# The folded pairs of a ConvFFN, written out by hand for four engines, with weight buffers in separate pools

## The chip, the core and the metric

The kernel runs on one core of a Trainium2 chip. The metric is the time of one execution on the device, in microseconds; several executions are timed and their median is taken. TensorE is called PE below (PEld is its weight load), VectorE DVE, ScalarE ACT, GpSimd POOL and SyncE SP. SP does nothing but issue loads and stores here; POOL does some arithmetic and issues the accumulating transfers named below.

## The reference

It is a trunk of two layers with width 1024 on one sequence of 512 positions. Each layer has a token mixer (retention in layer 0, mLSTM in layer 1) and a channel mixer, the ConvFFN, both behind an RMSNorm whose shift, scale and gate come from a vector `c`. The change is in the ConvFFN of layer 1, the last mixer before the final norm.

```python
D_MODEL, SEQ, DEPTH, D_FF, FFN_CONV = 1024, 512, 2, 2816, 3

def conv_ffn(h, w_up, conv_w, conv_b, w_down):
    u = causal_dwconv(h @ w_up, conv_w, conv_b)        # 5632 columns, three taps in time
    a, b = jnp.split(u, 2, axis=-1)
    return (jax.nn.silu(a) * b) @ w_down

for i in range(DEPTH):
    ...
    x = x + gt_t * mixer(h)
    h = rmsnorm(x, norm_ffn_g[i]) * (1.0 + sc_f) + sh_f
    x = x + gt_f * conv_ffn(h, ffn_w_up[i], ffn_conv_w[i], ffn_conv_b[i], ffn_w_down[i])
return rmsnorm(x, final_g)
```

## The kernel before

**Arithmetic.** Every large product is taken in three parts. A float32 matrix is split into a rounded high part and a remainder, its low part, and PE multiplies high by high, high by low and low by high (`mm3`, L231 to L233). A weight arrives as a tile of 128x1024 floats, `raw`, 512 KB, loaded on SP's queue. ACT casts it into `whi` (L155) and DVE subtracts that from `raw` into `wlo` (L160). There is a second way to a low part, `low_part_added`: ACT writes minus `whi` into `wlo` (L166), and a DMA on POOL's queue adds the weight to it (L167).

**Straight pairs and folded pairs.** The up-projection has 44 tiles of 128 columns; tile f and tile f + 22 make a pair, since the Silu of the one gates the other. A straight pair is two chains of 24 matmuls over 512 positions. A folded pair is worked out as a matrix of 2x2 blocks with seven block products in place of eight: a product is 12 matmuls over 256 positions, so a pair has 84 of them. The seven need sums of the two weight tiles (`wa`, `wb` give `ws` and `wt`, L205 to L208 on DVE), the same kind of sums of `h` (made once, in `turn`), and additions afterwards. `c1` and `c2` are two PSUM banks of 128x512. Three times ACT copies half of `c2` out: `s[HA]` after product 1 (L348), `s[HB]` after product 6 (L339), `q` after product 7 (L343), and DVE adds a copy into a bank (L340, L344, and the one behind product 3). Product 6 accumulates onto what product 1 left in `c2`, so it can't start ahead of the copy of `s[HA]`; product 7 stands so to the copy of `s[HB]`, and product 4 to the addition of `q` (L344). Products 1 and 2 take the parts of `wa`, 5 and 7 those of `ws`, 6 and 3 those of `wt`; product 4 takes `bp`, a tile that holds the high and the low part of half of `wb` side by side.

**What follows a pair.** For each of its two tiles ACT starts the convolution out of the bank (L748) and DVE adds two taps (L750). Then ACT takes the Silu (L760), DVE multiplies the halves (L761), ACT casts the result into `ggh` (L227) and DVE subtracts for `ggl` (L228). This is called the gate of a pair here. The down-projection runs in pieces over groups of 4, 4, 4, 4 and 6 pairs; a piece is one tile of `w_dn` with 24 matmuls over 512 positions in two halves of 12, each followed by the addition to the residual x (L419).

**Order.** The program is a list of items, each with the weights that it uses. Weights go out up to four items ahead, as long as a budget of tiles allows. All tiles of weights, whatever they hold, come from one pool, `wts`, of 22 buffers that go round in turn: a buffer is given out again once its last reader is done. Pairs 0 to 3 are straight and 4 to 21 folded (`FOLD_FROM`). A folded pair is an item of its own, `fold_item`, called a unit here; in 16 of the 18 units a piece of `w_dn` is run between the products (`down`, from the second unit on). Inside a unit PE's order is that of the code. The order on ACT, DVE and POOL is set by the scheduler, which ranks ready instructions by their place in the program. The unit's parameter `prepare` holds the steps for the next fold: `step_a` (parts of `wa`, all sums), `step_b` (parts of `ws`), `step_c` (parts of `wt`, with the accumulating DMA in every second fold), `step_d` (`bp`), and last the load of the fold after next. The last group of six is run behind all units by `boundary`, in two halves of the positions, with the final norm beside it.

Of the kernel before, what the change touches and what calls it, by code (L numbers as in the profile page):

```python
# [9 lines left out]
F32 = mybir.dt.float32  # L10
# [17 lines left out]
NWT = 22  # L28
BUDGET = 16
BUDGET_FOLD = 20  # L30
FOLD_FROM = 4
# [8 lines left out]
NSLOTS = 58  # L40
# [30 lines left out]
def trunk(ctx: ExitStack, tc: tile.TileContext, xT, cb, pos, vec, decay, zmask, ada, w_s0, w_in0, w_v0,  # L71
# [4 lines left out]
    wts = ctx.enter_context(tc.tile_pool(name="wts", bufs=NWT))  # L76
# [13 lines left out]
    def wide(s, dt=F32):  # L90
        return wts.tile([P, WCOLS + WPAD], dt, tag="w", name=s)
# [21 lines left out]
    c_ext = const.tile([P, D + 1], F32, tag="c", name="c_ext")  # L113
# [8 lines left out]
    V.memset(const.tile([P, 32], F32, tag="pad2", name="pad2")[:], 0.0)  # L122
# [47 lines left out]
    class Chunk:  # L170
        tiles = 2

        def __init__(self, src, n, off):
            raw, r = wide(uid("raw")), slice(0, n)
            nc.sync.dma_start(raw[:, r], src)
            self.hi = high_part(raw, r, off)
            self.lo = low_part(raw, self.hi, r, off)

    class Fold:


        tiles = 7

        def __init__(self, src, n, off):
            pass

        def load(self, src):
            self.a, self.b = wide(uid("wa")), wide(uid("wb"))
            nc.sync.dma_start(self.b[:, :WCOLS], src[1])
            nc.sync.dma_start(self.a[:, :WCOLS], src[0])  # L190
            self.p = {}

        def both(self, w, low, i, j):
            r = slice(0, WCOLS)
            hi = high_part(w, r, OFF)
            lo = low(w, hi, r, OFF)
            self.p[i], self.p[j] = (hi, 0, lo, 0), (hi, T, lo, T)

        def step_a(self):
            a, b = self.a, self.b  # L200
            f = lambda t, i: t[:, i * T : i * T + T]
            self.s13, self.s24 = wide(uid("ws")), wide(uid("wt"))
            s13, s24 = self.s13, self.s24
            self.both(a, low_part_added, 1, 2)
            V.tensor_tensor(f(s13, 0), f(b, 0), f(b, 1), op=ALU.add)  # L205
            V.tensor_tensor(f(s13, 1), f(a, 0), f(b, 0), op=ALU.subtract)
            V.tensor_tensor(f(s24, 0), f(s13, 0), f(a, 0), op=ALU.subtract)
            V.tensor_tensor(f(s24, 1), f(a, 1), f(s24, 0), op=ALU.subtract)  # L208

        def step_b(self):  # L210
            self.both(self.s13, low_part_added, 5, 7)

        def step_c(self, added):
            self.both(self.s24, low_part_added if added else low_part, 6, 3)

        def step_d(self):
            bp = wide(uid("wb"), F32R)[:, OFF : OFF + WCOLS]
            A.copy(bp[:, :T], self.b[:, T:WCOLS])
            V.tensor_tensor(bp[:, T:], self.b[:, T:WCOLS], bp[:, :T].bitcast(F32), op=ALU.subtract)
            self.p[4] = (bp, 0, bp, T)  # L220
# [76 lines left out]
    class Use:  # L297


        def __init__(self, src, n, kind=Chunk, off=0):  # L300
            self.src, self.n, self.first, self.kind, self.off = src, n, None, kind, off

    def item(uses, fn, free=True):
# [4 lines left out]
        items.append((uses, fn, free))  # L308

# [11 lines left out]
    def fold_item(fold, h, terms, thens, down, prepare):  # L321


        def fn(w):
            p, c1, c2 = fold.p, bank("p1"), bank("p2")
            s, q = slot("fs"), slot("fq")

            def product(i, o, start=False):
                hi, hc, lo, lc = p[i]
                for k in range(4):  # L330
                    b = terms(i, k)
                    st, sp = start and k == 0, i in (2, 3, 4) and k == 3
                    ch, cl = slice(hc + k * P, hc + k * P + P), slice(lc + k * P, lc + k * P + P)
                    PE.matmul(o, hi[:, ch], b[0], start=st, stop=False, skip_group_check=True)  # L334
                    PE.matmul(o, hi[:, ch], b[1], start=False, stop=False, skip_group_check=True)
                    PE.matmul(o, lo[:, cl], b[0], start=False, stop=sp, skip_group_check=True)  # L336

            def u2():
                A.copy(s[:, HB], c2[:, HA])  # L339
                V.tensor_tensor(c1[:, HA], c1[:, HA], s[:, HA], op=ALU.add)  # L340

            def u3():
                A.copy(q[:, HA], c2[:, HA])  # L343
                V.tensor_tensor(c2[:, HB], c1[:, HB], q[:, HA], op=ALU.add)  # L344
            product(1, c2[:, HA], True)
            if down:
                product(5, c1[:, HB], True)
                A.copy(s[:, HA], c2[:, HA])  # L348
                prepare[0]()
                product(2, c1[:, HA])  # L350
                product(6, c2[:, HA])
                u2()
                prepare[1]()
                down[1](w[1], 0, T, js=(0,))
                product(7, c2[:, HA])
                u3()
                prepare[2]()
                down[1](w[1], 0, T, js=(1,))
            else:
                product(2, c1[:, HA], True)  # L360
                A.copy(s[:, HA], c2[:, HA])
# [970 lines left out]
```

## Time and profile before

| What | Value |
|---|---|
| Three timed runs | 1691.68, 1694.57, 1696.71 us; median 1694.57 |
| The profiled execution | 1694.29 us, with a span of 1692.5 us |
| Granted TensorE clock, mean | 0.970 |
| Busy share of PE, DVE, ACT, POOL | 93%, 67%, 46%, 11% |
| Folded pairs, from the first matmul of the first to the last of the last | 1267.7 to 1653.5 us |

The profile is of one execution, and its instructions have times from the span's start; 1.8 us of the execution lie around the span. A granted clock below 1 means that PE ran at a lower speed for a part of the time. The rows by window give for each engine the busy time and the number of instructions. The rows of waits read: engine, tile and line that waited, what it waited for, then total us, count and median us. In the rows by line, `x18 | 7.7, 429 | 12.2` means 18 instructions, 7.7 us busy, 429 ns each in the mean, and 12.2 us of idle time ahead of them. In the rows in order of time come the start in us, the duration in us, then engine, line, operation and tiles; an idle time ahead of the instruction stands in brackets at the end.

### The profile page before, as it was taken

How to read it: one execution, taken by the hardware profiler on the slowest of the kernel's cores; microseconds unless marked ns; L12 is line 12 of the kernel's file. 1: busy time of each engine (PE TensorE's matmuls, PEld its weight loads, DVE VectorE, ACT ScalarE, POOL GpSimd, SP SyncE). 2: the span in 40 equal slices, each digit the busy share in tenths (PEclk: the TensorE clock that was granted, in tenths of full speed). 3: DMA queues.
4: the chain of work that ended last, by engine and by line, in shares of the span. 5: the costliest groups of instructions: out<-in, count | busy, mean ns of one | idle time of the engine just before them, and what ended most of it. 6: DMA issues, size and time to landing. Idle time of an engine off the chain costs nothing.

```text
span 1692.5 us, 21688 instructions
## 1 busy us (share of the span) xinstructions
PE 1572.4 (93%) x8464; PEld 1358.7 (80%) x8464; DVE 1140.3 (67%) x1638; ACT 775.2 (46%) x1149; POOL 185.0 (11%) x197
## 2 busy tenths in 40 slices
PE   7999999998999999999999999999997778778797
PEld 4688888888888877889988888888986777677687
DVE  8976785868887677645766867557895555455555
ACT  4435334343553234424645635444565444555443
POOL 4221011100200000001101110101121001111002
PEclk9999999999999999999999999999998888988999
DMA  9334435442265554232232322222235555555531
GB/s 349 124 146 154 149 138 193 162 169 99 88 210 177 197 188 149 100 112 87 77 126 75 113 87 100 75 95 80 76 81 136 133 137 137 137 132 134 139 94 51
DMA packets 66314, 220.20 MB, mean 130 GB/s; under 512 B 9106, under 2 KB 11410, under 8 KB 66211
## 3 DMA queue, kind: packets, MB, share of 16 engines
q1 hardware_dynamic: 59730, 195.22, 32.6%
q0 software_dynamic: 6480, 23.60, 7.4%
q8 instruction: 66, 1.08, 0.3%
q14 instruction: 38, 0.30, 0.1%
HBM read 193.06 MB, written 2.12 MB: 115 GB/s over the span
## 4 chain that ended last, share of the span: by engine, by line
PE 69%; DVE 11%; DMA 9%; issue 7%; ACT 4%; SPq 0%; POOL 0%; DVEq 0%; ACTq 0%; POOLq 0%
PE pp L233 10%; PE pp L232 10%; PE pp L231 10%; PE po L231 6%; PE po L233 6%; PE po L232 6%; DMA raw<-w_dn 4%; PE pv L407 3%; PE pv L406 3%; PE pv L408 3%; DMA wlo<-wa 2%; DVE wlo L160 2%; DMA wlo<-ws 2%; ACT whi L155 2%; DVE cv L750 1%
## 5 line engine op out<-in xcount | busy, mean ns | idle before, releaser
L160 DVE TENSOR_TENSOR wlo<-raw,whi 128x1024 fp32r<-128x1024 f32 (+1 forms) x222 | 269.6, 1217 | 135.5 <-ACT whi L155 100.4
L233 PE MATMUL pp<-hh,wlo 128*128 128x512 f32 x816 | 318.6, 391 | 2.6 <-DVE wlo L160 2.6
L232 PE MATMUL pp<-hl,whi 128*128 128x512 f32 x816 | 317.6, 389 | 0.0
L231 PE MATMUL pp<-hh,whi 128*128 128x512 f32 x816 | 317.4, 389 | 0.0
L155 ACT CAST whi<-raw 128x1024 fp32r<-128x1024 f32 (+1 forms) x222 | 226.3, 1029 | 103.2 <-DMA raw<-w_dn 44.8
L419 DVE SCALAR_TENSOR_TENSOR x<-po,mod,x 128x512 f32<-128x512 f32 (+1 forms) x168 | 102.4, 619 | 123.2 <-PE po L233 123.0
L233 PEld LDWEIGHTS pp<-hh,wlo 128*128 128x128 f32 x816 | 153.1, 188 | 38.3 <-DVE wlo L160 6.9
L232 PEld LDWEIGHTS pp<-hl,whi 128*128 128x128 f32 x816 | 153.2, 188 | 31.8
L231 PEld LDWEIGHTS pp<-hh,whi 128*128 128x128 f32 x816 | 153.1, 188 | 31.3
L231 PE MATMUL po<-ggh,whi 128*128 128x512 f32 (+1 forms) x464 | 161.5, 351 | 0.1
L232 PE MATMUL po<-ggl,whi 128*128 128x512 f32 (+1 forms) x464 | 161.1, 348 | 0.0
L233 PE MATMUL po<-ggh,wlo 128*128 128x512 f32 (+1 forms) x464 | 159.7, 345 | 0.6 <-DVE wlo L160 0.6
L233 PE MATMUL po<-yh,wlo 128*128 128x256 f32 (+1 forms) x352 | 116.2, 332 | 3.8 <-DVE wlo L160 3.8
L231 PE MATMUL po<-yh,whi 128*128 128x256 f32 (+1 forms) x352 | 116.5, 332 | 0.8 <-ACT whi L155 0.8
L232 PE MATMUL po<-yl,whi 128*128 128x256 f32 (+1 forms) x352 | 116.3, 331 | 0.0
L132 DVE SCALAR_TENSOR_TENSOR ada<-ada,c_ext 128x1025 f32<-128x1025 f32 x93 | 114.6, 1237 | 0.0
L233 PEld LDWEIGHTS po<-ggh,wlo 128*128 128x128 f32 x464 | 90.3, 195 | 12.1 <-DVE wlo L160 1.0
L231 PEld LDWEIGHTS po<-ggh,whi 128*128 128x128 f32 x464 | 91.0, 197 | 10.1 <-ACT ggh L227 0.3
L232 PEld LDWEIGHTS po<-ggl,whi 128*128 128x128 f32 x464 | 91.1, 196 | 9.1
L750 DVE SCALAR_TENSOR_TENSOR cv<-pp,vecs,cv 128x511 f32<-128x511 f32 (+1 forms) x88 | 65.4, 748 | 43.9 <-ACT cv L748 42.6
L334 PE MATMUL p<-t24h,whi 128*128 128x256 f32 x72 | 27.9, 388 | 69.9 <-ACT fs L348 69.9
L336 PE MATMUL p<-hh,wlo 128*128 128x256 f32 x288 | 81.8, 284 | 6.1 <-DMA wlo<-ws 6.1
(283 smaller groups left out, 3368.2 us busy)
## 6 DMA issues: line engine op xcount, KB each, us to landing
ada<-ada SPq DMA_DIRECT2D x96, 512.5 KB, 3.6
raw<-w_in SPq DMA_DIRECT2D x62, 512.0 KB, 3.3
raw<-w_up SPq DMA_DIRECT2D x52, 512.0 KB, 3.7
raw<-w_o SPq DMA_DIRECT2D x32, 512.0 KB, 3.4
raw<-w_dn SPq DMA_DIRECT2D x32, 512.0 KB, 3.3
raw<-w_v SPq DMA_DIRECT2D x28, 512.0 KB, 3.2
wb<-w_up SPq DMA_DIRECT2D x18, 512.0 KB, 5.8
wa<-w_up SPq DMA_DIRECT2D x18, 512.0 KB, 4.6
```

The costliest lines, as they stand in the source:

```text
L132: return V.scalar_tensor_tensor(raw, raw, 1.0, c_ext[:], op0=ALU.mult, op1=ALU.mult, accum_out=mods[layer][:, f : f + 1])
L155: A.copy(hi, w[:, r])
L160: V.tensor_tensor(lo, w[:, r], hi.bitcast(F32), op=ALU.subtract)
L231: PE.matmul(o, ah, bh, start=start, stop=False)
L232: PE.matmul(o, ah, bl, start=False, stop=False)
L233: PE.matmul(o, al, bh, start=False, stop=stop)
L336: PE.matmul(o, lo[:, cl], b[0], start=False, stop=sp, skip_group_check=True)
L406: PE.matmul(pss[t][:], h[k].hi[:, cs], w[0].hi[:, ws], start=st, stop=False)
L407: PE.matmul(pss[t][:], h[k].hi[:, cs], w[0].lo[:, ws], start=False, stop=False)
L408: PE.matmul(pss[t][:], h[k].lo[:, cs], w[0].hi[:, ws], start=False, stop=sp)
L419: V.scalar_tensor_tensor(x[m][:, r], ps[:, r], gate_col, x[m][:, r], op0=ALU.mult, op1=ALU.add)
L750: V.scalar_tensor_tensor(acc[:, s:], ps[:, : T - s], c(j), acc[:, s:], op0=ALU.mult, op1=ALU.add)
```

## The change

It replaces the one pool by three: `whi` and `wlo` tiles of split weights, 8 buffers each, and 8 buffers `raw` of 128x1025 floats for raw weights, `wa`, `wb`, the sums, the columns of `c`'s projection (`ada`) and the output. `bp` becomes a `whi` tile, and `c_ext`, a constant tile of its own before, now holds a buffer of `raws` while the projections of `c` run. In place of the budget, weights go out ahead when a buffer of `whi` eight uses back is through (`Ahead`). Pair 4 becomes straight, so that 17 pairs are folded. The `w_dn` pieces run in units 0 to 15 of 17. The pool of 128x512 tiles has 57 in place of 58.

The units become one function, `folded`, in which the order of PE, DVE, ACT and POOL is that of the code. The gate of the pair before is taken apart (`steps`) and stands in pieces inside the next unit, and the splits of the next fold stand between them. The order of the products and half pieces on PE within a unit stays as it was. The loads of the fold after next and of the `w_dn` tile for the unit after next are issued at the unit's end. `turn`, which makes the sums of `h`, moves behind the last straight product.

```diff
-NWT = 22
-BUDGET = 16
-BUDGET_FOLD = 20
-FOLD_FROM = 4
+WBUFS = 8
+RAWS = 8
+FOLD_FROM = 5
...
-NSLOTS = 58
+NSLOTS = 57
...
-    wts = ctx.enter_context(tc.tile_pool(name="wts", bufs=NWT))
+    wpool = ctx.enter_context(tc.tile_pool(name="wpool", bufs=WBUFS))
+    raws = ctx.enter_context(tc.tile_pool(name="raws", bufs=RAWS))
...
     def wide(s, dt=F32):
-        return wts.tile([P, WCOLS + WPAD], dt, tag="w", name=s)
+        if dt == F32:
+            return raws.tile([P, D + 1], F32, tag="raw", name=s)
+        return wpool.tile([P, WCOLS + WPAD], dt, tag=s[:3], name=s)
...
-    c_ext = const.tile([P, D + 1], F32, tag="c", name="c_ext")
+    c_ext = wide("c_ext")
...
-            bp = wide(uid("wb"), F32R)[:, OFF : OFF + WCOLS]
+            self.bp = wide(uid("whi"), F32R)[:, OFF : OFF + WCOLS]
...
+        def may(self, n):
+            u = self.flat[self.at]
+            if any(n <= b < u.first for b in bars):
+                return False
+            return u.first <= n + AHEAD and (self.at < WBUFS or self.flat[self.at - WBUFS].last < n)
...
+        def unit(i):
+            f = folds[i + 1] if i + 1 < len(folds) else None
+            d = chunks[i + 1] if i + 1 < len(downs) else None
+            with_down = i < len(downs)
+            at = pairs[i - 1] if i else None
+            if at:
+                last(i - 1)
+                at.init(1, banks[i - 1][1])
+                at.init(0, banks[i - 1][0])
+            c1, c2 = banks[i] = bank("p1"), bank("p2")
+            s, q = sums[i] = slot("fs"), slot("fq")
+            product(i, 1, c2[:, HA], True)
+            if at:
+                at.taps(1)
+            if with_down:
+                product(i, 5, c1[:, HB], True)
             else:
...
+            A.copy(s[:, HA], c2[:, HA])
+            if f:
+                f.high_a()
+                f.sums_13()
+                f.low_a()
...
+            if at:
+                at.taps(0)
+            if with_down:
+                product(i, 2, c1[:, HA])
+            if f:
+                f.high_13()
+            if at:
+                at.silu()
+            V.tensor_tensor(c1[:, HA], c1[:, HA], s[:, HA], op=ALU.add)
+            if at:
+                at.gate()
+            product(i, 6, c2[:, HA])
+            A.copy(s[:, HB], c2[:, HA])
+            if f:
+                f.low_13()
+                f.sums_24()
...
+            if at:
+                at.high()
+                at.low()
+            if with_down:
+                down(i, 0)
...
+            if f:
+                f.high_24()
+                f.low_24(i % 2)
...
+            product(i, 7, c2[:, HA])
+            A.copy(q[:, HA], c2[:, HA])
+            V.tensor_tensor(c2[:, HB], c1[:, HB], q[:, HA], op=ALU.add)
+            if d:
+                d.high()
+                d.low()
+            down(i, 1)
+            if f:
+                f.high_b()
+                f.low_b()
...
+            product(i, 4, c2[:, HA])
+            product(i, 3, c1[:, HB])
+            if i + 2 < len(folds):
+                folds[i + 2].load()
+            load_down(i + 2)
...
-                early(self.start.turn, first[4], first[5])
...
+                proj_item(w[4 + FT], self.h, lambda ps: (self.start.turn(), th(ps)))
+                bars.append(len(items))
+                item([], run)
```

In `run`, the function around `unit`, all units stand under one manual order for the four engines, and the gate of the last pair follows the last unit. The steps have the names of their work: `high_a` and `low_a` are the parts of `wa`, `sums_13` and `sums_24` make `ws` and `wt`, `high_13`, `low_13`, `high_24` and `low_24` are the parts of these, `high_b` and `low_b` make `bp`, `d.high` and `d.low` the parts of the next `w_dn` tile. `low_24` is done by the accumulating DMA in units with an odd number and by DVE in the others.

What stands on ACT in a unit from the middle of the stage is shown first. Before, from the first part of `bp` to the split of the next `wa` (`cv` are the convolution's tiles, `p` the banks):

```order
L218 CAST wb_12867<-wb_12714 128x512
L748 ACTIVATE cv_12699<-p_2251_12553,vecs 128x512
L748 ACTIVATE cv_12703<-p_2252_12554,vecs 128x512
L760 ACTIVATE cv_12699<-cv_12699 128x512
L227 CAST ggh_12709<-cv_12699 128x512
L155 CAST whi_12892<-raw_12890 128x1024
L348 COPY fs_12728<-p_2276_12727 128x256
L155 CAST whi_12929<-wa_12885 128x1024
L166 ACTIVATE wlo_12931<-whi_12929 128x1024
```

Now, from the start of such a unit (L424 is the copy of `s[HA]`, L444 that of `s[HB]`; L879 starts the convolution, L905 is the Silu, L913 the gate's cast):

```order
L879 ACTIVATE cv_12110<-p_2169_11946,vecs 128x512
L879 ACTIVATE cv_12112<-p_2168_11945,vecs 128x512
L424 COPY fs_12116<-p_2193_12115 128x256
L157 CAST whi_12145<-wa_12103 128x1024
L168 ACTIVATE wlo_12150<-whi_12145 128x1024
L157 CAST whi_12167<-ws_12147 128x1024
L905 ACTIVATE cv_12112<-cv_12112 128x512
L444 COPY fs_12116<-p_2193_12115 128x256
L168 ACTIVATE wlo_12185<-whi_12167 128x1024
L913 CAST ggh_12191<-cv_12112 128x512
L157 CAST whi_12209<-wt_12188 128x1024
L168 ACTIVATE wlo_12211<-whi_12209 128x1024
```

The copy of `s[HA]` stood behind the Silu and the cast of the gate before, and behind the cast of a `w_dn` tile; it now stands behind the two convolution starts, and Silu and gate's cast are behind it.

SP's queue in two units, with what each load waits for (a count of finished instructions of an engine; `DMAHW` is the end of a load, `DMASW` that of an accumulating DMA). Before:

```order
L189 DMA wb_12369<-w_up 128x1024 [waits DMASW7_49,DMAHW3_49,DMASW3_49,PE_49]
L190 DMA wa_12368<-w_up 128x1024 [waits DMASW7_49,DMAHW4_49,DVE_49,Activation_49]
L175 DMA raw_12373<-w_dn 128x1024 [waits PE_49]
L189 DMA wb_12541<-w_up 128x1024 [waits DMAHW6_49,PE_49]
L190 DMA wa_12540<-w_up 128x1024 [waits DMAHW7_49,DMASW5_49,DVE_49]
L175 DMA raw_12545<-w_dn 128x1024 [waits DMAHW3_49,DMAHW0_49,DVE_49]
```

Now:

```order
L192 DMA wb_12104<-w_up 128x1024 [waits DMAHW4_49,DMAHW0_49,DVE_49]
L193 DMA wa_12103<-w_up 128x1024 [waits DMASW3_49,DMASW1_49,DMASW0_49]
L175 DMA raw_12107<-w_dn 128x1024 [waits DMAHW2_49,DVE_49]
L192 DMA wb_12274<-w_up 128x1024 [waits DMASW7_49,DMASW3_49,DMAHW3_49,DVE_49,Activation_49]
L193 DMA wa_12273<-w_up 128x1024 [waits DMAHW7_49,DVE_49]
L175 DMA raw_12277<-w_dn 128x1024 [waits DMAHW5_49,DVE_49]
```

The three loads of a unit stand in the same order; PE is no longer among what they wait for.

On DVE, before, a stretch from the gate's low part (L228) to the second residual of a `w_dn` piece (L419):

```order
L228 TENSOR_TENSOR ggl_12537<-cv_12526,ggh_12536 128x512
L340 TENSOR_TENSOR p_2251_12553<-p_2251_12553,fs_12555 128x256
L160 TENSOR_TENSOR wlo_12722<-raw_12718,whi_12720 128x1024
L419 SCALAR_TENSOR_TENSOR x_84<-po_12624,mod_107,x_84 128x512
L205 TENSOR_TENSOR ws_12755<-wb_12714 128x512
L344 TENSOR_TENSOR p_2252_12554<-p_2251_12553,fq_12556 128x256
L206 TENSOR_TENSOR ws_12755<-wa_12713,wb_12714 128x512
L207 TENSOR_TENSOR wt_12756<-ws_12755,wa_12713 128x512
L208 TENSOR_TENSOR wt_12756<-wa_12713,wt_12756 128x512
L419 SCALAR_TENSOR_TENSOR x_85<-po_12657,mod_107,x_85 128x512
```

Now, from the addition of `s[HA]` (L440) to the low part of `bp` (L239); L550 is the residual, L466 the addition of `q`:

```order
L440 TENSOR_TENSOR p_2168_11945<-p_2168_11945,fs_11947 128x256
L909 TENSOR_TENSOR cv_11943<-cv_11943,cv_11941 128x512
L218 TENSOR_TENSOR wt_12019<-ws_11978,wa_11934 128x512
L219 TENSOR_TENSOR wt_12019<-wa_11934,wt_12019 128x512
L917 TENSOR_TENSOR ggl_12023<-cv_11943,ggh_12022 128x512
L550 SCALAR_TENSOR_TENSOR x_89<-po_12026,mod_110,x_89 128x512
L162 TENSOR_TENSOR wlo_12042<-wt_12019,whi_12040 128x1024
L466 TENSOR_TENSOR p_2169_11946<-p_2168_11945,fq_11948 128x256
L162 TENSOR_TENSOR wlo_12060<-raw_11938,whi_12058 128x1024
L550 SCALAR_TENSOR_TENSOR x_90<-po_12062,mod_110,x_90 128x512
L239 TENSOR_TENSOR whi_12076<-wb_11935,whi_12076 128x512
```

The gate's product and low part and the sums `wt` now stand in one unit at fixed places, and the addition of `q` (L466) stands behind a whole low part of `wt` (L162) in every second unit, where the sums stood around it before (L344).

More of the change, by code (lines that the diff above doesn't have):

```diff
@@ L815, in items @@
             for gi, n in enumerate(groups):
-                ahead = base + n + 2 if gi < len(groups) - 2 else FT
-                while nxt < min(ahead, FT):
+                upto = base + n + 2 if gi < len(groups) - 2 else FT
+                while nxt < min(upto, FT):
                     self.up(nxt)
```

305 lines of the change are left out of this document (176 added, 129 removed).

## Prediction

> **What bounds the kernel now.** I read the page first, then the work by windows, then the waits of the last mixer, then its instructions in order of time.
>
> ```profile
> span 1692.5 us, 21688 instructions
> PE 1572.4 (93%) x8464; PEld 1358.7 (80%) x8464; DVE 1140.3 (67%) x1638; ACT 775.2 (46%) x1149; POOL 185.0 (11%) x197
> PEclk9999999999999999999999999999998888988999
> ```
>
> TensorE (PE) is busy for 93% of the span, but the granted clock drops in the last quarter. The windows say what that quarter holds (columns: length, then busy time and instructions of PE, PEld, DVE, ACT, POOL, then clock, DMA share, GB/s).
>
> ```profile
> 0.00:100.00 100.00, 85.11 (x307) 60.59 (x308) 84.43 (x117) 42.62 (x65) 32.40 (x23) 0.95 0.55 206
> 900.00:1100.00 200.00, 200.00 (x940) 168.83 (x939) 136.45 (x181) 104.18 (x155) 23.88 (x27) 1.00 0.25 87
> 1267.70:1653.50 385.80, 304.64 (x1948) 280.17 (x1948) 204.20 (x311) 189.83 (x260) 36.13 (x42) 0.89 0.51 130
> ```
>
> Between 900 and 1100 us PE never rests and its clock is 1.00. From the first to the last matmul of the folded pairs, 1267.7 to 1653.5, it rests for 385.8 - 304.6 = 81.2 us, at a clock of 0.89. No other engine is near its limit there: DVE is busy for 53%, ACT for 49%, the DMA engines for 51%. Who makes PE wait:
>
> ```profile
> PE p L334 <- ACT fs L348: 69.9, 16, 7.0
> PE p L336 <- DMA wlo<-ws: 6.1, 1, 6.1
> PE p L334 <- DVE p L344: 5.0, 3, 2.4
> ACT whi L155 <- DMA raw<-w_dn: 33.6, 17, 4.7
> SPq L189 <- PE p L336: 221.9, 14, 19.9
> ```
>
> The three PE rows make 81.0 us, all of its idle time. 69.9 us is one instruction, the first copy of a unit (L348), which must read the bank before product 6 may add to it. Two units of ACT in order of time:
>
> ```profile
> 1487.65 1.43 ACT L748 ACTIVATE cv<-p,vecs 128x512 f32<-128x512 f32 x2
> 1490.61 0.63 ACT L760 ACTIVATE cv<-cv 128x512 f32<-128x512 f32 x1 [1.02 <-DVE cv L750]
> 1492.41 0.62 ACT L227 CAST ggh<-cv 128x512 fp32r<-128x512 f32 x1 [1.17 <-DVE cv L761]
> 1492.93 0.36 ACT L348 COPY fs<-p 128x256 f32<-128x256 f32 x1
> 1516.73 1.04 ACT L155 CAST whi<-raw 128x1024 fp32r<-128x1024 f32 x1 [0.66 <-DMA raw<-w_dn]
> 1517.68 0.36 ACT L348 COPY fs<-p 128x256 f32<-128x256 f32 x1
> ```
>
> The copy stands behind the whole gate of the pair before (convolution, DVE taps, Silu, product, cast), and in every second unit also behind the cast of a `w_dn` tile that is still landing. That tile is late because SP's queue stands still: the load of `wb` waited 221.9 us for the last product 4 or 3, whose operand lies in a buffer of the same pool.
>
> **The change, term by term.** The spacing of matmuls gives PE's price; warm 256 columns (12 steps in 1.41 us), warm 512 columns (16 steps in 3.62), and 256 columns after a wait (14 rows from 1505.56):
>
> ```profile
> 1511.52 0.28 PE L336 MATMUL p<-hh,wlo 128*128 128x256 f32 x1
> 1512.93 0.28 PE L336 MATMUL p<-hh,wlo 128*128 128x256 f32 x1
> ...
> 1254.62 0.39 PE L233 MATMUL pp<-hh,wlo 128*128 128x512 f32 x1
> 1258.24 0.39 PE L231 MATMUL pp<-hh,whi 128*128 128x512 f32 x1
> ...
> 1504.35 0.39 PE L334 MATMUL p<-t24h,wb 128*128 128x256 f32 x1 [2.44 <-DVE p L344]
> 1505.56 0.42 PE L334 MATMUL p<-t24h,wb 128*128 128x256 f32 x1
> 1508.55 0.41 PE L336 MATMUL p<-hh,wlo 128*128 128x256 f32 x1
> ```
>
> So 0.1175, 0.2263 and about 0.213 us. The stage's 1948 matmuls are 18 x 84 = 1512 of folded pairs, 16 x 24 = 384 of `w_dn` pieces, and 52 of the boundary behind it. Warm and without a gap they need 1512 x 0.1175 + 384 x 0.2263 + 52 x 0.1175 = 177.7 + 86.9 + 6.1 = 270.7 us. Of 385.8 us, then, 81.2 are idle and 304.6 - 270.7 = 33.9 are the slow clock behind the idle: **115.1 us** in all, the most that a better order of these units can give.
>
> One folded pair becomes a straight one: 48 x 0.2263 - 84 x 0.1175 = 10.9 - 9.9 = **+1.0**.
>
> A unit then needs 9.87 + 5.43 = 15.3 us of PE. Can the others keep up? Their prices (mean ns) and the landing of the accumulating DMAs:
>
> ```profile
> L750 DVE SCALAR_TENSOR_TENSOR cv<-p,vecs,cv 128x511 f32<-128x511 f32 (+1 forms) x68 | 46.4, 745 | 15.0 <-ACT cv L748 15.0
> L228 DVE TENSOR_TENSOR ggl<-cv,ggh 128x512 fp32r<-128x512 f32 x19 | 13.2, 692 | 10.4 <-ACT ggh L227 10.3
> L419 DVE SCALAR_TENSOR_TENSOR x<-po,mod,x 128x512 f32<-128x512 f32 x32 | 23.9, 747 | 41.2 <-PE po L233 41.1
> L160 DVE TENSOR_TENSOR wlo<-wt,whi 128x1024 fp32r<-128x1024 f32 x8 | 9.8, 1224 | 18.8 <-ACT whi L155 18.8
> L344 DVE TENSOR_TENSOR p<-p,fq 128x256 f32<-128x256 f32 x18 | 7.7, 429 | 12.2 <-ACT fq L343 12.2
> L166 ACT ACTIVATE wlo<-whi 128x1024 fp32r<-128x1024 f32 x42 | 44.5, 1059 | 4.8 <-DVE wlo L160 2.8 <-ACT whi L155 0.4
> L155 ACT CAST whi<-ws 128x1024 fp32r<-128x1024 f32 x17 | 17.9, 1050 | 26.7 <-PE po L232 19.6 <-DVE ws L206 7.2
> L748 ACT ACTIVATE cv<-p,vecs 128x512 f32<-128x512 f32 x34 | 24.5, 769 | 10.3 <-DVE p L373 10.3
> L227 ACT CAST ggh<-cv 128x512 fp32r<-128x512 f32 x19 | 11.7, 618 | 16.2 <-DVE cv L761 16.2
> L339 ACT COPY fs<-p 128x256 f32<-128x256 f32 x18 | 6.7, 373 | 34.2 <-PE p L336 34.2
> L167 POOL DMA_DIRECT2D wlo<-wa x18: 850/859/1051, 1227.5 to 1616.5; - x18
> DMA to landing us min/median/max: 4.4/6.2/8.5
> ```
>
> Where a row isn't shown, a 512-wide DVE operation counts as L228's 0.69 and a 512-wide one of ACT as L227's 0.62. DVE's fixed list in a unit is 4 taps, 7 operations of 0.69 (four sums, gate, two low parts), 3 of 0.43, 2 of 0.75 and one or two low parts of 1.22: 11.8 us, or 13.0 in every second unit. ACT's is 2 x 0.77 + 3 x 0.37 + 4 x 1.05 + 2 x 1.06 + 3 x 0.62 = 10.8, or 11.9 with a third multiply. Both are below 15.3. The fixed order then has to bring three things to PE in time, counted from the start of product 1:
>
> - The first copy now stands behind two convolution starts only: done at 1.8, wanted by product 6 at 4.2.
> - The second copy has in front of it on ACT a cast, a multiply, a cast (until 5.0) and the Silu, which waits for DVE (0.43 + 1.49 + 1.37 + 1.49 = 4.8): Silu until 5.45, product 6 until 5.65, copy until 6.05. Product 7 wants it at 5.65 + 2.72 = 8.4: 2.3 us to spare.
> - The third copy follows product 7 (9.8) and ends at 10.2, its DVE addition at 10.85, since DVE is held by the low part that starts when the residual's addition ends (9.2 + 1.22). Product 4 wants it after the second half piece, at 12.5: 1.65 to spare.
>
> The accumulate into `wlo` from `ws` starts after the multiply at 7.1 and, at the longest landing of before, is there at 15.6; product 5 of the next unit reads it at 15.3 + 1.65 = 16.95. The loads no longer wait for PE: raw weights have 8 buffers of their own, a unit takes 5, so those of the fold after next start about when a unit starts, a whole unit ahead. The DMA engines' share goes from 0.51 at 21.9 us per unit to some 0.7. So I take each unit as PE's own 15.3, plus the smallest wait that the order of before leaves on this path, L344's 5.0 us over 18 units = 0.28 each: 16 units, **+4.5** (bounds: 0, as between 900 and 1100 us; and 1.9, below).
>
> The turn of `h` now stands behind the last straight product. On ACT follow four 256-wide casts, a Silu, a convolution start, then DVE's taps and product, and the cast of the gate, all ahead of the first copy: 4 x 0.37 + 0.62 + 0.77 + 1.49 + 0.69 + 0.62 + 0.37 = 6.0 us, where product 6 is reached at some 4.2: a stall of about 2, and, since a wait of 2.44 us was followed by 3.2 us at half speed in the rows above, 1.5 more: **+3.5** (0 to 6.1, the first unit's wait now). The Trainium skill ("TensorE: Matmul & The Clock Gate", "What's actually happening") halves the clock only after an idle window of about 3.4 us; by it the 1.5 would fall away and the sum be lower by that. The rows disagree, a shorter wait was enough, so I keep the 1.5. The last unit has no `w_dn` piece, but matmuls of the boundary stand between its product 7 and 4, as now: 0.
>
> Elsewhere the pools are split: raw weights get 8 tiles, one held by `c_ext`. Only the start is short of tiles, where loads that went out ahead now wait for DVE. DVE is busy for 84% of the first 100 us and paces it; the loads keep about two steps of lead. 0 to +5, I take **+1**. One slot less moves a few loads; 0, since PE has no gap there to lengthen.
>
> The sum, against the profiled execution's own 1694.3 (the median, 1694.57, is 0.3 above it): 1694.3 - 115.1 + 1.0 + 4.5 + 3.5 + 1.0 = **1589 us**.
>
> **The rivals.**
> 1. DVE paces the unit. It has only 2.3 us to spare, and in before it waited for ACT's results (L750, L228, L344) 15.0 + 10.4 + 12.2 = 37.6 us, 2.1 per unit. Once, that gives 15.1, still covered; twice, 17.2, so +1.9 in 16 units: 1589 + 30 = 1619. For it: strict order on both engines. Against it: the slack above.
> 2. The accumulates land late, as three DMAs per unit now share 15.3 us with the loads. Up to 9.8 us are covered; at 12 each unit waits 2.2: 1589 + 35 = 1624. A rule of the Trainium skill speaks for it ("SBUF — State Buffer", "SBUF: two separate sides"): GpSimd can't write its descriptors while DVE holds their shared port, and DVE's share rises from 0.53 to 0.81. Against it: issue took 850 to 1051 ns over all 18 rows, so the trace shows no such stall.
> 3. The change doesn't do what it says, and ACT still stands behind something late at each first copy: half of the loss stays, 1589 + 57 = 1646. Against: neither cast nor gate is ahead of that copy now.
> 4. Slower: the buffers of raw weights come free a unit later than I read, so that a unit becomes one chain from the last low part (14.2) over load (some 5), cast 1.05, multiply 1.06 and accumulate 6.2, or 27.5 us: 1589 + 12.2 x 16 = 1784. It turns into a loss at 15.3 + 105/16 = 21.9 us per unit. Against: the loads wait for readers one unit back.
>
> **How the numbers follow.** The forecast 0.70 (its own range 1577 to 1605: all bounds low, with up to 4 us of the other idle time gone, and 1 us per unit over), rival 1 0.13, rival 2 0.08, rival 3 0.05, rival 4 0.03, no change 0.01. Up to 1622 lie the forecast and most of rival 1, 8 in 10: 1577 to 1622. Within 0.3% (5 us), about what a measurement here can tell from nothing: 0.01; faster 0.96; slower 0.03.
>
> **What would show it.** Right: in the folded stage no wait of PE for a copy over 1 us but one at its start, a clock of 0.98 or more, product 1 every 15.3 us, SP's loads waiting for DVE, ACT or accumulates. Wrong: a row of PE waiting for `wlo` by DMA (rival 2), for the addition behind the third copy (rival 1), or DVE and ACT waiting for loads in every unit (rival 4).

## The result, and the profile after

The changed kernel took 1569.75 us in the median of four runs (1568.99 to 1570.65), the kernel before 1693.71 beside it: a ratio of 0.927 (95% interval 0.925 to 0.928). The forecast was 1589 with a range of 1577 to 1622. The direction came out, and in the folded stage the mechanism too, but the gain was some 18 us larger than the sum, and the time lies below the range. The page of the changed kernel, whose profiled execution took 1570.65 us:

```profile
span 1568.8 us, 21573 instructions
PE 1539.3 (98%) x8428; PEld 1336.7 (85%) x8428; DVE 1136.2 (72%) x1631; ACT 772.1 (49%) x1142; POOL 186.2 (12%) x195
PEclk8999999999999999999999999999999999999999
```

The drop of the clock in the last quarter is gone. The folded stage by windows (columns as before), and all waits of PE over 1 us in the whole span (the third number in a row of waits is the longest of them, not the median, here and in the rows ahead of this section):

```profile
1267.60:1525.30 257.70, 257.70 (x1825) 241.81 (x1824) 193.79 (x289) 176.04 (x244) 34.46 (x40) 1.00 0.71 178
...
PE pst L1141 <- ACT hh L306: 7.3, 4, 3.7
PE pf L252 <- DVE hl L308: 4.0, 4, 1.3
PE pms L256 <- ACT ssh L247: 2.7, 2, 1.5
PE pc L1099 <- DMA c_row<-cb: 2.4, 1, 2.4
PE pst L1143 <- DVE hl L308: 1.8, 1, 1.8
```

PE is busy for all of the 257.7 us, at full clock, and no row names a folded product any more. A unit takes 15.39 us. The three copies on ACT (L444 and L465 in one unit, L424 in the next), with what stands ahead of them:

```profile
1410.13 1.03 ACT L157 CAST whi<-ws 128x1024 fp32r<-128x1024 f32 x1
1411.07 0.63 ACT L905 ACTIVATE cv<-cv 128x512 f32<-128x512 f32 x1
1412.05 0.37 ACT L444 COPY fs<-p 128x256 f32<-128x256 f32 x1 [0.36 <-PE p L389]
...
1416.21 0.37 ACT L465 COPY fq<-p 128x256 f32<-128x256 f32 x1 [0.28 <-PE p L389]
...
1422.25 0.78 ACT L879 ACTIVATE cv<-p,vecs 128x512 f32<-128x512 f32 x1 [1.10 <-DVE p L404]
1423.20 0.37 ACT L424 COPY fs<-p 128x256 f32<-128x256 f32 x1 [0.16 <-PE p L389]
```

and, from the same unit, DVE's addition of `q` and the first matmuls of products 7 and 4:

```profile
1416.62 0.43 DVE L466 TENSOR_TENSOR p<-p,fq 128x256 f32<-128x256 f32 x1 [1.07 <-ACT fq L465]
...
1414.60 0.28 PE L387 MATMUL p<-t3h,whi 128*128 128x256 f32 x1
1418.76 0.28 PE L387 MATMUL p<-t24h,whi 128*128 128x256 f32 x1
```

It is now the copies that wait for PE. The second is done at 1412.42 and product 7 starts at 1414.60: 2.2 us to spare, as the prediction had it (2.3); the addition ends at 1417.05, 1.7 ahead of product 4 (1.65 in the prediction).

But the folded stage is not all. One more straight pair now runs ahead of it, 10.9 us of PE, and yet its first product starts where it did. The product's row in both kernels (duration min/median/max, first and last start):

```profile
L334 PE MATMUL p<-hh,whi x288: 276/281/415, 1267.8 to 1653.1; 128*128 128x256 f32 x144
...
L387 PE MATMUL p<-hh,whi x272: 276/281/281, 1267.6 to 1525.0; 128*128 128x256 f32 x136
```

So 1267.8 - (1267.6 - 10.9) = 11.1 us were gained ahead of the stage. Where, the same stretch of the clock tells (386 to 440 holds the output projection of the retention mixer, which both kernels reach at 386.1 and 386.0; before first, then after):

```profile
386.00:440.00 54.00, 48.12 (x349) 45.26 (x348) 45.94 (x72) 22.82 (x40) 6.43 (x8) 0.97 0.28 98
564.00:721.00 157.00, 155.23 (x676) 125.91 (x675) 112.90 (x154) 64.18 (x83) 0.00 (x0) 1.00 0.44 149
...
386.00:440.00 54.00, 52.77 (x401) 50.46 (x401) 50.45 (x82) 27.14 (x51) 8.52 (x8) 1.00 0.37 124
564.00:721.00 157.00, 157.00 (x694) 130.07 (x693) 112.69 (x150) 66.14 (x84) 0.00 (x0) 1.00 0.48 154
```

Before, PE rested for 5.9 us in the first stretch, lost clock, and paused once per item in the second; after, it runs through. By the starts of like matmuls, the changed kernel was 8 to 9 us ahead after the first stretch, 13.1 after the second and 14.6 at most; 3.5 were given back in the mLSTM mixer and behind it, and I have no cause for these. Behind the projection's waits stands the loads' queue (SP in order of time; start, duration of the issue, then with `x5` several merged into one row; before, then after):

```profile
385.05 6.80 SPq L175 DMA_DIRECT2D raw<-w_o  x2
395.16 3.27 SPq L175 DMA_DIRECT2D raw<-w_up  x2
...
377.64 0.33 SPq L175 DMA_DIRECT2D raw<-w_o  x1
378.78 10.40 SPq L175 DMA_DIRECT2D raw<-w_up  x5
```

The last tile of `w_o` and the first of `w_up` go out 14 and 16 us earlier. What SP waited for up to the folded stage says why (before, then after):

```profile
SPq L175 <- PE pp L233: 240.5, 48, 13.2
SPq L175 <- DVE wlo L160: 150.0, 41, 13.6
SPq L175 <- PE po L233: 119.3, 22, 13.2
...
SPq L175 <- DVE wlo L162: 576.6, 127, 25.1
```

Loads waited for matmuls in the whole kernel, not in the folded stage alone. With pools apart SP waits for a matmul once up to the folded stage, for 1.1 us; nearly all of its waits are for DVE.

### The profile page after: what moved, and what is told of

Same layout as the page of the kernel before. It is cut to its first block, busy times and chain, and to the rows that moved or that the text cites. A ratio compares the mean times of both kernels' runs of the same rounds, so it can differ in the third digit from the quotient of the medians.

```text
span 1568.8 us, 21573 instructions
## 1 busy us (share of the span) xinstructions
PE 1539.3 (98%) x8428; PEld 1336.7 (85%) x8428; DVE 1136.2 (72%) x1631; ACT 772.1 (49%) x1142; POOL 186.2 (12%) x195
## 5 line engine op out<-in xcount | busy, mean ns | idle before, releaser
L162 DVE TENSOR_TENSOR wlo<-raw,whi 128x1024 fp32r<-128x1024 f32 (+1 forms) x224 | 271.5, 1214 | 135.2 <-ACT whi L157 133.8
L157 ACT CAST whi<-raw 128x1024 fp32r<-128x1024 f32 (+1 forms) x224 | 230.7, 1033 | 259.7 <-PE pp L252 95.9
L251 PE MATMUL pp<-hh,whi 128*128 128x512 f32 x832 | 323.9, 389 | 0.5 <-DVE vl L248 0.5
L252 PE MATMUL pp<-hl,whi 128*128 128x512 f32 x832 | 323.8, 389 | 0.0
L253 PE MATMUL pp<-hh,wlo 128*128 128x512 f32 x832 | 323.7, 389 | 0.0
L550 DVE SCALAR_TENSOR_TENSOR x<-po,mod,x 128x512 f32<-128x512 f32 (+1 forms) x168 | 102.5, 618 | 95.8 <-PE po L253 95.7
L252 PE MATMUL po<-ggl,whi 128*128 128x512 f32 (+1 forms) x464 | 156.2, 337 | 0.0
L251 PE MATMUL po<-ggh,whi 128*128 128x512 f32 (+1 forms) x464 | 155.7, 337 | 0.1
L251 PEld LDWEIGHTS po<-ggh,whi 128*128 128x128 f32 x464 | 87.1, 188 | 8.9 <-ACT ggh L913 0.3
L538 PE MATMUL pv<-wlo,hh 128*128 128x512 f32 x224 | 87.2, 389 | 0.0
L539 PE MATMUL pv<-whi,hl 128*128 128x512 f32 x224 | 87.0, 389 | 0.0
L537 PE MATMUL pv<-whi,hh 128*128 128x512 f32 x224 | 87.0, 389 | 0.0
```

The lines of the kernel that those rows point to most:

```text
L157: A.copy(hi, w[:, r])
L162: V.tensor_tensor(lo, w[:, r], hi.bitcast(F32), op=ALU.subtract)
L251: PE.matmul(o, ah, bh, start=start, stop=False)
L252: PE.matmul(o, ah, bl, start=False, stop=False)
L253: PE.matmul(o, al, bh, start=False, stop=stop)
L537: PE.matmul(pss[t][:], h[k].hi[:, cs], w[0].hi[:, ws], start=st, stop=False)
```

## The experiments

First the parts of the change were taken apart, then single prices were measured. Each run has runs of the kernel before beside it on the same chip; those had medians of 1694.7 to 1697.8. The first mark of the table is the start of the retention mixer's output projection, up to which all kernels do the same (runs differ there by up to 3 us), the second the first folded product; the third column is their distance, brought to four straight pairs by taking 10.9 off for each further one. "Stage" is from the first to the last start of the product's row above, which holds 18, 17 or 16 folded pairs.

| Kernel | median us | mark 1 | mark 2 | ahead of stage | stage |
|---|---|---|---|---|---|
| before | 1693.71 | 386.1 | 1267.8 | 881.7 | 385.3 (18) |
| after | 1569.75 | 386.0 | 1267.6 | 870.7 | 257.4 (17) |
| before, pools alone | 1676.78 | 387.5 | 1258.6 | 871.1 | 378.5 (18) |
| after, one pool | 1581.82 | 387.0 | 1278.5 | 880.6 | 257.6 (17) |
| after, copy behind gate | 1634.25 | 385.4 | 1266.9 | 870.6 | 321.9 (17) |
| after, PE alone by hand | 1578.10 | 384.8 | 1266.3 | 870.6 | 266.4 (17) |
| before, gate later | 1606.20 | 386.8 | 1269.4 | 882.6 | 292.1 (18) |
| before, gate later and pools | 1581.01 | 385.8 | 1256.5 | 870.7 | 280.7 (18) |

**The pools alone in the kernel before.**

```diff
-    wts = ctx.enter_context(tc.tile_pool(name="wts", bufs=NWT))
+    wpool = ctx.enter_context(tc.tile_pool(name="wpool", bufs=WBUFS))
+    raws = ctx.enter_context(tc.tile_pool(name="raws", bufs=RAWS))
...
-            bp = wide(uid("wb"), F32R)[:, OFF : OFF + WCOLS]
+            bp = wide(uid("whi"), F32R)[:, OFF : OFF + WCOLS]
```

> The kernel before with the three pools alone (bp a whi tile, c_ext in raws, 57 tiles of 128x512); planner, fold_item and the scheduler's order stay. Theory A (outside the folded pairs the gain of 11 us comes from loads that no longer wait for PE): the first folded product starts at 1257 us in place of 1267.8. Inside the folded pairs the copy of s[HA] stays behind the gate, but no longer behind a cast of a w_dn tile that is landing: PE's waits for it fall from 69.9 to some 35 to 45 us and the stage from 385.8 to some 335 to 350, so the whole to 1635 to 1650 us. Rival B (the gain outside comes from the new rule by which weights go out ahead): the first folded product stays at 1267 to 1268, the whole at 1645 to 1660. Rival C (only the hand-written order counts): 1690 or more.

Measured: 1676.78 us, ratio 0.988 (0.986 to 0.990). Ahead of the stage the whole 10.6 us came, so theory A held there with the old planner and the old rule. Inside I was wrong: 7 us in place of 35 to 50.

```profile
PE p L338 <- ACT fs L352: 64.9, 16, 8.4
```

The copy still comes 4 us late in a unit (64.9 / 16), and it stands right behind the gate's cast:

```profile
1504.26 0.62 ACT L231 CAST ggh<-cv 128x512 fp32r<-128x512 f32 x1 [1.94 <-DVE cv L765]
1504.79 0.36 ACT L352 COPY fs<-p 128x256 f32<-128x256 f32 x1
```

ACT waits for no load of a `w_dn` tile there any more, so the gate alone makes the copy late. Units that alternated between some 20 and some 24 us now mostly take 20.6 to 20.9; why the shorter ones became longer is open.

**One pool again in the changed kernel.**

```diff
-        if dt == F32:
-            return raws.tile([P, D + 1], F32, tag="raw", name=s)
-        return wpool.tile([P, WCOLS + WPAD], dt, tag=s[:3], name=s)
+        return wpool.tile([P, WCOLS + WPAD], dt, tag="w", name=s)
```

(with 22 buffers in the one pool, and `c_ext` a constant tile again)

> The changed kernel with one pool of 22 buffers again (c_ext a constant tile), order by hand kept. Theory A: the 11 us outside are lost again, the first folded product moves from 1267.6 to 1278 or 1279. Inside, loads wait for product 7 of the unit before, some 7 us ahead of their casts with a landing of 4 to 5, so the units stay near 15.4 us: 1580 to 1590 us in all. Rival B (rule for going ahead, not pools): the first folded product stays at 1267 to 1268 and the whole at 1570 to 1575. Rival D (the hand-written order lives on the pools): units of 18 us or more, 1620 or more.

Measured: 1581.82 us, 12 more than with the pools, as theory A had it. Ahead of the stage 9.9 us are lost again, and such rows of PE's waits and of SP's come back, while the units stay at 15.39 us. The order by hand, then, doesn't depend on the pools.

```profile
PE po L250 <- DVE wlo L159: 4.6, 4, 2.9
...
SPq L172 <- PE pp L250: 240.1, 47, 13.2
```

**Raw weights apart, high and low parts together.** One more run of the pools:

```diff
-        return wpool.tile([P, WCOLS + WPAD], dt, tag=s[:3], name=s)
+        return wpool.tile([P, WCOLS + WPAD], dt, tag="w", name=s)
```

(with 16 buffers in that pool)

> The changed kernel with the raw weights in their own pool of 8 as now, but high and low parts together in one pool of 16. Theory A (what counts outside the folded pairs is that a load no longer takes a buffer that PE must first have read): no change, the first folded product at 1266 to 1268 and the whole at 1568 to 1573. Rival (high and low parts apart matter): the first folded product later by several us, up to 1582.

Measured: 1572.79 us. It is 3 us slower, but its marks are 387.3 and 1269.1, 870.9 ahead of the stage: of the 2 us that its profiled execution lost, 1.3 lie ahead of mark 1, where the runs differ anyway. It is the raw weights' own buffers that count.

**The copy back behind the gate.** In the changed kernel:

```diff
-            A.copy(s[:, HA], c2[:, HA])
             if f:
                 f.high_a()
...
             if at:
                 at.silu()
-            V.tensor_tensor(c1[:, HA], c1[:, HA], s[:, HA], op=ALU.add)
             if at:
                 at.gate()
+                at.high()
+                at.low()
+            A.copy(s[:, HA], c2[:, HA])
+            V.tensor_tensor(c1[:, HA], c1[:, HA], s[:, HA], op=ALU.add)
             product(i, 6, c2[:, HA])
             A.copy(s[:, HB], c2[:, HA])
...
-            if at:
-                at.high()
-                at.low()
```

> The changed kernel with the copy of s[HA] moved back behind the whole gate on ACT (behind Silu and the gate's cast, with the addition of s[HA] on DVE behind it); all else stays. Theory (the place of this copy made the 81.2 us idle and 33.9 us of slow clock): the gate's chain ends some 6.1 us into a unit, product 6 wants the copy at 4.2, so PE waits 1.9 us in 16 units, 30 us; if such a wait also halves the clock for some 3.2 us, as behind the wait of 2.44 us in the profile of before, 1.5 us more each: 1600 to 1625 in all. If only waits over 3.4 us halve the clock, 1600. Rival (the late w_dn tile was the cause, not the place of the copy): under 1580.

Measured: 1634.25 us, 64.5 more, above the range of the theory and far from that of the rival.

```profile
PE p L387 <- ACT fs L443: 42.7, 17, 2.7
...
1267.10:1589.00 321.90, 279.18 (x1830) 256.59 (x1830) 194.24 (x292) 174.60 (x242) 33.56 (x39) 0.94 0.57 141
```

The waits are 2.67 us long in 15 units, where I had 1.9, and PE is busy for 279.2 us where the changed kernel has 257.7: 21.5 us more, on top of 42.7 idle. By the trace's records of the clock, half speed was granted 11 times, and a unit with such a spell is 1.6 us longer (17.23 against 15.63 us of PE, in the rows under "The clock" below), which makes 17.6. The rest is some 0.24 us for each wait, paid at full clock too (15.63 against 15.39). The place of one copy, with the addition that follows it, is worth half of the whole gain.

**The copy behind three operations of ACT only.**

```diff
-            A.copy(s[:, HA], c2[:, HA])
             if f:
                 f.high_a()
...
             if f:
                 f.high_13()
+            A.copy(s[:, HA], c2[:, HA])
             if at:
                 at.silu()
```

> The changed kernel with the copy of s[HA] moved behind three operations of ACT only (both parts of wa and the high part of ws, 3.1 us), ahead of the Silu. The copy then ends some 5.3 us into a unit, where product 6 wants it at 4.2: a wait of 1.0 to 1.2 us in 16 units, 16 to 19 us. If a wait of that length never halves the clock: 1586 to 1590. If the clock is halved behind some of them, as behind waits of 2.5 us in 12 of 16 units with the copy behind the whole gate: 1595 to 1610.

Measured: 1578.58 us, 8.8 more.

```profile
PE p L387 <- ACT fs L437: 5.0, 15, 0.3
...
1266.40:1532.80 266.40, 261.34 (x1825) 242.14 (x1824) 195.62 (x291) 172.97 (x242) 33.59 (x39) 1.00 0.67 170
```

The copy ended some 0.6 us earlier than the durations add up to, 4.7 us into a unit, and the clock stayed at 1.00. A wait of 0.33 us made a unit 0.56 us longer, the same 0.23 or so on top of the idle time.

**Order by hand for PE alone.** In the changed kernel:

```diff
-            with tc.manual_schedule(engines={mybir.EngineType.PE, mybir.EngineType.DVE, mybir.EngineType.Activation,
-                                             mybir.EngineType.Pool}):
+            with tc.manual_schedule(engines={mybir.EngineType.PE}):
```

> The changed kernel with PE alone in hand-written order; ACT, DVE and POOL are ranked by the scheduler again, but from the new code with its small steps and pools. Theory (what counts is that gate and splits are small steps that stand at the right place in the program, so that the copy is not behind the Silu): within 15 us of the changed kernel, 1570 to 1585. Rival (the order on ACT and DVE has to be fixed by hand): units of 18 to 21.9 us again, 1615 to 1680.

Measured: 1578.10 us, 8.4 more; the theory held. All units but the first take 15.2 to 15.7 us. The first takes 23.0, with the stall that I had forecast for the change and a spell of slow clock behind it:

```profile
PE p L387 <- ACT fs L424: 4.0, 1, 4.0
```

**The gate one unit later, in the kernel before.** The convolution, Silu and split of a pair are put into the program behind the next unit's first copy, and nothing else is changed:

```diff
                 A.copy(s[:, HA], c2[:, HA])
+                gate_before()
                 prepare[0]()
...
-            thens[0](c1)
-            thens[1](c2)
+            waiting.append(lambda: (thens[0](c1), thens[1](c2)))
```

> The kernel before with one edit: the gate of a folded pair is put into the program behind the copy of s[HA] of the next unit, in place of the end of its own. One pool, 18 folded pairs, the scheduler's order on ACT, DVE and POOL stay. Theory (the place of this copy is what cost the folded stage; order by hand on four engines isn't needed for it): the waits for the copy go from 69.9 us to under 10 and the clock recovers, so the whole comes to 1580 to 1605 us, the 11 us outside being left. Rival (w_dn tiles that land late stand ahead of the second copy now and make it late in its turn): waits of 2 to 3 us for the second copy in every second unit or more, 1610 to 1650.

Measured: 1606.20 us, ratio 0.946 (0.945 to 0.948): some three quarters of the gain from one edit, a microsecond above what I expected. No wait for a copy is left; what is left inside is the accumulating DMA, most likely late since loads still wait for PE: with the pools, in the next run, its waits are gone but for one.

```profile
PE p L342 <- DMA wlo<-ws: 11.5, 8, 5.9
PE p L342 <- DMA wlo<-wt: 3.5, 1, 3.5
```

**The same with the pools.**

> The same edit together with the three pools. Theory: both gains add up, the first folded product starts at 1257 to 1259 and the stage has units of 15.4 to 16 us: 1568 to 1585. Rival (the order by hand of all four engines carries a part of the gain of its own): 1590 or more.

Measured: 1581.01 us, 25 less than without the pools: 12 ahead of the stage, 11 inside. From the last two products of the second unit on, PE rests for only 0.9 us. The first two units, up to there, need 144 x 0.1175 + 24 x 0.2263 = 22.4 us and took 32.8, with 7.4 us of waits and a clock of 0.90; this is nearly all of the 11 us by which this kernel is behind the changed one. Which part of the change removes it (the order by hand, the piece in the first unit, the earlier `turn`) was not taken apart:

```profile
1256.40:1289.20 32.80, 25.40 (x170) 23.69 (x170) 20.34 (x35) 19.74 (x31) 3.44 (x4) 0.90 0.51 121
1289.20:1520.80 231.60, 230.72 (x1621) 215.89 (x1620) 172.52 (x263) 156.32 (x220) 31.93 (x38) 1.00 0.76 189
```

**All low parts on DVE, and all by DMA.** Two runs against rivals 1 and 2; in the second `low_24` is always accumulated.

```diff
-            self.low(self.a, low_part_added, 1, 2)
+            self.low(self.a, low_part, 1, 2)
...
-            self.low(self.s13, low_part_added, 5, 7)
+            self.low(self.s13, low_part, 5, 7)
...
-            self.low(self.s24, low_part_added if added else low_part, 6, 3)
+            self.low(self.s24, low_part, 6, 3)
```

> The changed kernel with every low part of the folds made by DVE, no accumulating DMA (two to three more subtractions of 1.22 us per unit). DVE's fixed list in a unit becomes 13.0 + 2.44 = 15.5 us against 15.39 of PE. Rival 1's mechanism (DVE paces the unit): at least 0.1 us more per unit, 2 us in all; if DVE also waits for ACT as often as once per unit in the profile of before (2.1 us), 17.6 us per unit and 35 us more, with slow clock up to 60: 1572 to 1630, most likely 1600. If DVE's order had slack that the sum doesn't see: 1570 to 1572.

> The changed kernel with the low part of wt made by the accumulating DMA in every unit, in place of every second (eight more DMAs, three per unit; DVE has 1.22 us less in those units). Theory (accumulates land 9 us before they are read, DVE has slack): within 2 us of the changed kernel, 1568 to 1572. Rival 2's mechanism (three accumulates and the loads get in each other's way): PE waits for wlo by DMA, 1575 to 1600.

Measured: 1569.82 and 1569.96 us, no change in either. The stage in both:

```profile
1267.20:1525.20 258.00, 257.49 (x1824) 236.92 (x1824) 233.02 (x330) 138.68 (x204) 0.00 (x0) 1.00 0.29 97
...
1267.00:1524.70 257.70, 257.70 (x1826) 241.83 (x1825) 185.55 (x281) 184.74 (x253) 41.41 (x48) 1.00 0.80 194
```

DVE busy for 90% of the stage, or the DMA engines for 80%, and PE waits for neither.

**One folded pair less.**

```diff
-FOLD_FROM = 5
+FOLD_FROM = 6
```

(with the items ahead of the units moved on by one pair)

> The changed kernel with one more straight pair (16 folded pairs, pair 5 straight). By the prediction's term 48 x 0.2263 - 84 x 0.1175 = +1.0 us: 1570.5 to 1572. Rival (at full speed a folded pair costs as much as a straight one, or its unit without a piece costs more): 1568 to 1570.

Measured: 1570.75 us, 1.0 more, though the two medians come from different runs of the chip and 1.0 us is near their spread. It speaks for the term of +1.0, not strongly.

No version beat the changed kernel.

## Why the prediction was wrong, step by step

Right was the core: 115.1 us of idle and slow clock in the folded stage could be got back, and the cause was the place of the first copy. The run with the gate later shows it by itself: 93 us of the stage from that one edit. The terms of the sum came to this:

| Term | predicted | measured |
|---|---|---|
| idle and slow clock of the stage | -115.1 | -115.1, with the next line |
| wait left per unit, 16 x 0.28 | +4.5 | +1.5 (257.7 against 1428 x 0.1175 + 384 x 0.2263 + 13 x 0.1175 = 256.2) |
| one pair straight | +1.0 | about +1 |
| stall at the start | +3.5 | 0 |
| pools, outside the stage | +1.0 | -11.1 |

From 1694.3 the measured terms lead to 1570.6, the profiled execution's 1570.65.

**The step that failed is the last term.** "Only the start is short of tiles ... 0 to +5, I take +1" let the pools cost something outside the stage and gain nothing. The same shared pool whose effect on SP I had read inside the stage (221.9 us for product 4 or 3) held up the queue everywhere, 240.5 us for `pp` in the kernel before alone. The waits of PE that this left were small ones in many places, 4.4 us for `po` and 2.6 for `pp` among them: up to 1246 us PE rested for 29.6 us in the kernel before and for 20.0 in the changed one, and the other 1.5 us of the 11.1 are most likely the slow clock between 386 and 440. I summed only the stage in which the waits were large, gave no reason that excluded a gain elsewhere, and left no more than 4 us for it in the lower bound. The runs with pools alone and with one pool show the 10 to 11 us come and go with the pools, with either planner and either order.

**The stall at the start** was 3.5 us by a chain in which four casts of `turn` and one Silu followed the last straight product. ACT in that place:

```profile
1263.87 1.00 ACT L247 CAST hh<-xr 128x256 fp32r<-128x256 f32 x3
...
1270.90 0.62 ACT L247 CAST ggh<-cv 128x512 fp32r<-128x512 f32 x1 [2.33 <-DVE cv L928]
1271.42 0.37 ACT L424 COPY fs<-p 128x256 f32<-128x256 f32 x1
...
1271.84 0.39 PE L387 MATMUL p<-t24h,whi 128*128 128x256 f32 x1
```

The casts ran while PE was still on the straight tile, since they need only `xr`; a place in the program is a rank, not a time. The copy ended at 1271.79 and product 6 started at 1271.84. That it was so near is shown by the run with PE alone by hand, where ACT took other casts first and the stall was there, 4.0 us.

**The wait per unit** was carried over from L344 in the order of before; in the new order this addition comes in time, as the prediction's own slack had said; the wait should not have been carried over. Nor are the 33.9 us behind the idle time all slow clock: at 0.24 us for each of 20 waits, an estimate from the runs above, some 5 of them are the price of waiting at all.

**The rivals.** DVE as the pace (0.13) and late accumulates (0.08) had no price at all, even with more load than the change puts on them. Their chances rested on sums of durations: I listed 12.4 us per unit for DVE in the mean, and 15.5 with every low part on it. Seven units of the changed kernel and of that run, and two instructions of DVE that follow each other:

```profile
1326.44:1434.14 107.70, 107.70 (x757) 100.85 (x756) 82.87 (x124) 73.43 (x101) 14.64 (x17) 1.00 0.75 189
...
1326.40:1434.00 107.60, 107.34 (x756) 98.23 (x755) 98.86 (x141) 57.67 (x84) 0.00 (x0) 1.00 0.31 103
...
1423.57 0.68 DVE L213 TENSOR_TENSOR ws<-wb 128x512 f32<-128x512 f32 x1
1424.17 0.68 DVE L214 TENSOR_TENSOR ws<-wa,wb 128x512 f32<-128x512 f32 x1
```

DVE was busy for 82.87 / 7 = 11.8 and 98.86 / 7 = 14.1 us per unit. The second instruction starts 0.60 us after the first, whose duration is 0.68: a sum of durations counts the overlap twice. With 141 / 7 = 20 instructions per unit that is up to 1.6 us, an estimate that covers the 1.4 between 15.5 and 14.1. For the accumulates, each issue took 859 to 1053 ns, much as before, with DVE busy for 75% of the stage, so the stall that spoke for rival 2 doesn't show. A shortage of raw buffers (rival 4) was not tried with fewer buffers; no run here has a wait of PE for a load in the folded units.

**The clock.** The prediction held against the Trainium skill ("TensorE: Matmul & The Clock Gate", "What's actually happening") that a wait shorter than an idle window of 3.4 us can halve the clock. The run with the copy behind the gate bears the prediction out, and the measurement decides: no wait there was over 2.7 us, and some 17.6 us went to slow clock. Four units of that run, each with a wait of 2.67 us:

```profile
1329.30:1349.20 19.90, 17.23 (x109) 15.76 (x109) 11.21 (x18) 11.16 (x15) 2.58 (x3) 0.91 0.65 159
1349.20:1369.10 19.90, 17.23 (x109) 15.60 (x109) 12.26 (x19) 10.11 (x14) 1.73 (x2) 0.91 0.53 132
1369.10:1387.40 18.30, 15.63 (x109) 14.44 (x109) 11.21 (x18) 11.17 (x15) 2.58 (x3) 1.00 0.71 173
1387.40:1407.30 19.90, 17.23 (x109) 15.76 (x109) 12.29 (x19) 10.11 (x14) 1.72 (x2) 0.91 0.53 133
```

PE rests for 2.67 us in each (19.90 - 17.23, 18.30 - 15.63); in three of them the unit is 1.6 us longer at a clock of 0.91, in one it is not. By the trace's records of the clock all spells of half speed in that stage were 3.41 us long, 11 behind 16 waits of 2.5 to 2.7 us (not 12, as one of the expectations has it). Their starts are 20.5 or 37.5 us apart, 6 or 11 times 3.41, though the units repeat after 18.3 or 19.9: they lie on a grid of steps of 3.41 us that the work doesn't set. The Trainium skill ("TensorE: Matmul & The Clock Gate", "What's actually happening") says that its window runs freely and doesn't reset when a kernel starts, and these records agree. Where a wait lies on the grid decided its price: all 11 waits that put 1.9 us or more of idle time into one step were followed by a step at half speed, and none of the 5 that put 1.63 us or less into each. This is the count of one run; no run here was made to test it.

## What to carry to other kernels

When a change takes away a wait by giving a resource buffers of its own, look up that resource's waits over the whole span, not only in the stage where they hurt most: many small waits made 11 us here. Ask of an operation that opens the way for the bottleneck what is ahead of it in its queue: a copy of 0.37 us behind a pair's gate cost some 90 of 124 us, and moving the gate behind it in the program did most of what a hand-written order of four engines did. When an engine's budget is summed from durations, check it against its busy time in a window, since the sum counts overlaps twice.

## What was not expected of the hardware

Behind a wait of 2.5 to 2.7 us TensorE's clock was halved for 3.41 us in 11 of 16 cases, behind 15 waits of 0.33 us never. Each wait also cost PE some 0.24 us beyond its idle time. In the rows above, successive instructions of ACT and DVE overlap by 0.08 to 0.1 us, and DVE, listed at 15.5 us per unit, was busy for 14.1. And the DMA engines in use for 80% of the stage, or DVE for 90%, cost PE nothing that can be measured (1569.96 and 1569.82 us against 1569.75).
